# A seventh place for split weight factors, in the mixers' tile of values, and one hidden tile of FFN1's first half more by Strassen's scheme

## The chip, the cores and the metric

The kernel runs on one core of one Trainium2 chip, in one launch. The metric is the device time of an execution in microseconds. The kernel before takes 1800.26 us (median of 3 runs, 1800.17 to 1800.42).

## The reference

One step of a hybrid decoder layer: a SwiGLU FFN taken half, a mixer (a gated linear recurrence beside sliding-window attention), and a second such FFN. All is fp32. The model is 1024 wide, the FFN's hidden layer 2816; 1024 prompt tokens and 32 sample tokens are worked on.

```python
def swiglu_ffn(x, w_gate, w_up, w_down):
    return (jax.nn.silu(x @ w_gate) * (x @ w_up)) @ w_down
...
    x = x + 0.5 * swiglu_ffn(rms_norm(x, ffn1[0]), ffn1[1], ffn1[2], ffn1[3])
    y, h_last, new_conv, new_k, new_v = token_mixer(rms_norm(x, mix[0]), pos, h0, conv_buf,
                                                    k_cache, v_cache, win, mix[1:])
    x = x + y
    x = x + 0.5 * swiglu_ffn(rms_norm(x, ffn2[0]), ffn2[1], ffn2[2], ffn2[3])
```

The change touches only how the two FFNs' products are made.

## The kernel before

**Precision.** Each fp32 value is kept as a high part rounded to the matmul's type and a low part, the rest. A product then is three matmuls: high by high, high by low, low by high. Weights are split on the core: ACT copies the loaded weights into a high part, DVE subtracts it from them for the low part.

**Stages.** Tokens go in two halves, one of them 544 wide (512 and the 32 sample tokens), the other 512. The order of work on PE is: FFN1's first half (544), FFN1's second half together with the first mixer, FFN2's first half with the second mixer, FFN2's second half (544). An FFN half walks over 22 hidden tiles of 128 (f = 0 to 21): gate and up products of a tile, the evacuation to `h` = silu(gate) x up, its split; after f = 3, 6, 10, 14, 18 and at the end come the down products of a group of hidden tiles (a down block).

**Plain and Strassen.** A plain tile (`gu`) has two units of weights (gate, up), each 128 x 1024, loaded by SP as 512 KB (`raw<-w`), split by L460 (ACT) and L462 (DVE). In the 544-wide halves its matmuls go over two halves of 272 columns (L502, L503): 96 for a tile. A tile by Strassen's scheme in Winograd's form (`gu7`) takes both units at once: four loads of 256 KB (`fa<-w`, L396), four sums on DVE (L414), seven factors 128 x 512, and seven products of 12 matmuls (L936): 84 for a tile. The products come in the order P1, P5, P6, P3, P7, P2, P4. P1, P2 and P4 take loaded quarters of the weights, the other four take sums. Their inputs are four quarters of x and four sums of them, T1 to T4, made once (`factors_of`, subtractions L697, splits L676 on ACT and L678 on DVE). T4 of FFN1's first half is split only when PE has done the last plain tile: it lies over what these read. `ev7` (L883 to L892) and `copy_of` (L869) evacuate the products. FFN1's first half has `FIRST7` plain tiles and goes on by `gu7`; FFN2's second half has three plain tiles, then `gu7`, and its down blocks go by the same scheme from the second on (`down7`, L1079: 84 matmuls for two units, two pairs of units, so 168 for a block).

**The places for split factors.** `whi_t` and `wlo_t` hold six places of 512 columns, managed by `wslots`. A plain unit takes an aligned pair of them, a factor of a product a single one. `split_pair` fills a single place: the high part by ACT (L429), the low one by DVE (L437); only in FFN2's second half, where the first half has stored the low parts of the same weights to `wl` in HBM, those of P1, P2 and P4 come back by a load that POOL issues (L433, 256 KB, 87 in all). The place is free again when PE has read it for the last matmul of its product.

**Which place is taken.** `Banks._pick` decides:

```python
        if n == 2:
            c = [(max(f[i].t, f[i + 1].t), i) for i in range(0, self.n, 2) if i in f and i + 1 in f]
        else:
            c = [(i ^ 1 in f, t.t, i) for i, t in f.items()]
        return min(c) if c else None
```

For a single place the first thing compared is whether the place's partner (its number with the last bit turned) is free too; a place whose partner is in use comes first. Only then the time at which it comes free, then its number.

**What sets the order.** `Sched` runs generators that yield requests for an engine (`Req`: engine, estimated duration, what it depends on), always the one that can start first by its own estimates, and so fixes each engine's order of instructions when the kernel is built. A load from `wl` is put down there as 1.0 us on POOL and 3.5 us more to landing. On the chip the order stands and semaphores do the rest: the refill of a place waits for PE's last reader of its old contents, PE waits for the refill.

**The mixers' tile of values.** `vt` (128 x 5 x 4 x 64) holds the attention's values. It is written first at L1512 and L1519, in the mixers, and read last at L1615. In FFN1's first half and in FFN2's second half it lies unused.

Of the kernel before, what the change touches and what calls it, by code (L numbers as in the profile page):

```python
# [74 lines left out]
WARM = 10  # L75
ORDER = ((0, 1, 2, 3), (0, 1, 2, 3, "s"))
MODES = (None, "tanh", "tanh")
FIRST7 = 7
MAINCAP = 6
DBIAS = 0.8  # L80

# [142 lines left out]
def layer(ctx: ExitStack, tc, t):  # L224
# [8 lines left out]
    NBIG, NPF, NH, NRM, NRAW, NW, NMX, NLW = 26, 4, 5, 6, 2, 3, 4, 1  # L233
# [5 lines left out]
    whi_t = const.tile([128, 2 * NW, 512], F32R, name="whi")  # L239
    wlo_t = const.tile([128, 2 * NW, 512], F32R, name="wlo")  # L240
# [3 lines left out]
    vt = const.tile([128, 5, 4, 64], F32R, name="vt")  # L244
# [34 lines left out]
    raws, wslots, mxp, lws = Pool(range(NRAW)), Banks(2 * NW), Pool(range(NMX)), Pool(range(NLW))  # L279
# [128 lines left out]
    def sums(n):  # L408
# [3 lines left out]
        for i, (o, x, y, op) in enumerate(((a, u1, u2, OP.add), (b, a, g1, OP.subtract), (c, g2, b, OP.subtract), (u1, g1, u1, OP.subtract))):  # L412
            tk = yield Req("D", 0.6, tok["raw", n, 0])
            V.tensor_tensor(o, x, y, op)  # L414
            done(("sum", n, i), tk)

    def split_pair(n):

        yield Req("A", 0.0, tok["raw", n, 0])
        (g1, g2, u1, u2), (s1, s2, s3) = raw_of[n], sum_of[n]  # L420
        st, pool, names = pairs[n]
        src = {"P1": (g1, None), "P5": (s1, 0), "P6": (s2, 1), "P3": (s3, 2), "P7": (u1, 3), "P2": (g2, None), "P4": (u2, None)}
        wplace[n], left = {}, []
        for name in names:
            r, dep = src[name]
            tk = yield Req("A", 0.55, tok["raw", n, 0] if dep is None else tok["sum", n, dep], wslots.soon(), when=wslots.has())
            w = wplace[n][name] = wslots.get()
            hi, lo = whi_t[:, w], wlo_t[:, w]
            S.activation(hi, F(r, 0), AF.Copy)  # L429
            at = LO[name] if st == 3 else None  # L430
            if at:
                tkl = yield Req("G", 1.0, tok["wl", order[n + at[0]]], lat=3.5)
                G.dma_start(lo, t["wl"][order[n + at[0]] - U_FFN2, :, at[1]])  # L433
                tk = Tok(max(tk.t, tkl.t))
            else:
                tk = yield Req("D", 0.6, tk)
                V.tensor_tensor(lo, F(r, 0), f32(hi), OP.subtract)  # L437
            done(("w", n, name), tk)
            left.append(r)
            if tok["sum", n, 3].t is not None and tok["w", n, "P7"].t is not None:  # L440
                pool.put(tk, *left)
                left = []
# [335 lines left out]
    def ffn(st, g, st2, u0, mode, rslot=None, plain=NF, d7=False):  # L778
# [3 lines left out]
        w = wide(st, g)  # L782
# [114 lines left out]
        def gu7(f):  # L897

            while hs.n() < 1:
                yield Req("P", 0.0, when=hs.has())  # L900
            H[f] = hs.get()[0]
            n = unit()
            unit()
            yield Req("P", 0.0, pff.soon(2), when=pff.has(2))
            a = pff.get()[0]
            if kept(f):
                yield Req("P", 0.0, big.soon(), when=big.has())
            c = (big if kept(f) else pff).get()[0]
            bs = []
            z0, z1 = slice(0, CB), slice(CB, 2 * CB)  # L910

            plan7 = (("P1", 0, "x1a", "", ("m1", F(a, w)[:, z0])), ("P5", 1, "T1", "", ("m5", F(c, w)[:, z1])), ("P6", 0, "T2", "m1", ("mV", F(a, w)[:, z1])),
                     ("P3", 1, "x2b", "m5", None), ("P7", 0, "T3", "mV", ("mW", F(c, w)[:, z0])), ("P2", 2, "x2a", "", None), ("P4", 0, "T4", "mW", None))
            for i, (name, b, x, after, then) in enumerate(plan7):
                xs = [fx(st, x, k) for k in range(4)]
                deps = [tok["w", n, name]] + [d for _, _, d in xs]
                dur = 12 * (CB / 2400 + 0.0125)
                if after:
                    tk = yield Req("P", dur, *deps, tok[after, f])
                elif b == 0:  # L920
                    tk = yield Req("P", dur, *deps, banks.soon(), when=lambda: banks.has()() and main_out[0] < 8)
                    bs.append(banks.get())
                    main_out[0] += 1
                elif b == 1:
                    tk = yield Req("P", dur, *deps, banks.soon(2), when=lambda: banks.has(2)() and main_out[0] < 7)
                    bs += [banks.get(2)]
                    bs.insert(1, bs[1] + 1)
                    main_out[0] += 2
                else:
                    tk = yield Req("P", dur, *deps)  # L930
                wp = wplace[n][name]
                for k, (h, l, _) in enumerate(xs):
                    o = k * 128
                    wh, wl = whi_t[:, wp, o:o + 128], wlo_t[:, wp, o:o + 128]
                    for j, (u, v) in enumerate(((wh, h), (wh, l), (wl, h))):
                        PE.matmul(ps[:, bs[b], :CB], u, v, start=not after and k == j == 0, stop=k == 3 and j == 2, skip_group_check=bool(after))  # L936
                wslots.put(tk, wp)
                done((name, f), tk)
                if then:
                    sc.spawn(copy_of(bs[b], then[1], tk, then[0], f), 0)  # L940
                if i == 5:
                    sc.spawn(ev7(f, bs, a, c), 0)
            if f == NF - 1:
                xfree(st2, g)
                if st == 1 and not g:
                    xfree(1, 1)
# [98 lines left out]
        def down7(gi, i):  # L1045

            grp = GROUPS[gi]
            n = unit()
            unit()
            z0, z1 = slice(0, CB), slice(CB, 2 * CB)  # L1050
            dn, bs = [None] * 2, [[None] * 3 for _ in range(2)]
            spec = {"P1": (0, "x1a", "", "m1"), "P5": (1, "T1", "", "m5"), "P6": (0, "T2", "m1", "mV"), "P3": (1, "x2b", "m5", None),
                    "P7": (0, "T3", "mV", "mW"), "P2": (2, "x2a", "", None), "P4": (0, "T4", "mW", None)}
            for name in pairs[n][2]:
                b, x, after, then = spec[name]
                xs = [hx(grp, x, k) for k in range(2)]
                for j in range(2):
                    key = (gi, i, j)
                    deps = [tok["w", n, name]] + [d for _, _, d in xs]
                    dur = 6 * (CB / 2400 + 0.0125)  # L1060
                    if after:
                        tk = yield Req("P", dur, *deps, tok[after, key])
                    elif b == 0:
                        tk = yield Req("P", dur, *deps, banks.soon(), when=lambda: banks.has()() and main_out[0] < 8)
                        bs[j][0] = banks.get()
                        main_out[0] += 1
                    elif b == 1:
                        tk = yield Req("P", dur, *deps, banks.soon(2), when=lambda: banks.has(2)() and main_out[0] < 7)
                        bs[j][2] = banks.get(2)
                        bs[j][1] = bs[j][2] + 1  # L1070
                        main_out[0] += 2
                    else:
                        tk = yield Req("P", dur, *deps)
                    wp = wplace[n][name]
                    for k, (h, l, _) in enumerate(xs):
                        o = j * 256 + k * 128
                        wh, wl = whi_t[:, wp, o:o + 128], wlo_t[:, wp, o:o + 128]
                        for q, (u, v) in enumerate(((wh, h), (wh, l), (wl, h))):
                            PE.matmul(ps[:, bs[j][b], :CB], u, v, start=not after and k == q == 0, stop=k == 1 and q == 2, skip_group_check=bool(after))  # L1079
                    done((name, key), tk)  # L1080
                    if then:
                        to = {"m1": (0, z0), "mV": (0, z1), "mW": (1, z0), "m5": (2, z0)}[then]
                        sc.spawn(copy_of7(bs[j][b], dn, j, to, tk, then, key), 0)
                    if name == "P5":
                        sc.spawn(evd7(gi, 2 * i + j, bs[j], dn, key), 1)
                wslots.put(tk, wp)
            if i == 1:
                for f in grp:
                    hs.put(tk, H.pop(f))
# [812 lines left out]
    rslot = big.get()[0]  # L1902
    plan = ffn(1, 0, 2, 0, "late", rslot, plain=FIRST7) + merge(ffn(1, 1, 2, 0, MODES[1]), mixer(0))
    plan += merge(ffn(3, 0, 4, U_FFN2, MODES[2]), mixer(1))
# [13 lines left out]
    def free_rslot():  # L1918
        yield Req("D", 0.0, tok["s", 1, 0, FIRST7 - 1], *(tok["y", k] for k in range(4)))
        big.put(tok["s", 1, 0, FIRST7 - 1], rslot)  # L1920

# [177 lines left out]
```

## Time and profile before

| | |
|---|---|
| runs, median (3) | 1800.26 us |
| profiled execution, its own time | 1800.32 us |
| its span | 1798.3 us |
| PE busy | 1786.3 us, 11106 matmuls |
| DVE, ACT busy | 1298.0 us, 984.9 us |
| POOL's loads from `wl` | 87, 256 KB, median 3.7 us to landing |

The span goes from the first to the last instruction of the profiled execution; 2.0 us lie around it. A row of the groups names line, engine, operation, output and inputs, count, then busy time, mean ns of one, the idle time ahead and what ended most of it. In a timeline a row is the start, the length, the engine and line, and in brackets the idle time before it with what ended it. PE is the engine that is busy throughout; what another engine does costs time where PE waits for it.

### The profile page before, as it was taken

The numbers are of one execution on the slowest core, as the hardware profiler recorded it, in microseconds if no ns is written. First come the engines' busy times: TensorE is split into PE (matmuls) and PEld (weight loads), VectorE is DVE, ScalarE is ACT, GpSimd is POOL, SyncE is SP. The second block draws the span as 40 slices with busy tenths as digits, with TensorE's granted clock in tenths as the row PEclk, the third lists the DMA queues.
The fourth block names the chain that finished last, engine by engine and source line by source line (L and its number), as shares of the span: only waits on it lengthen the run. The fifth ranks groups of instructions, "written<-read, shape, count | busy, mean of one in ns | idle before, by whom it ended". The sixth has DMA issues, their size and how long they took to land.

```text
span 1798.3 us, 28694 instructions
## 1 busy us (share of the span) xinstructions
PE 1786.3 (99%) x11106; PEld 1627.8 (91%) x11106; DVE 1298.0 (72%) x2218; ACT 984.9 (55%) x1685; POOL 61.7 (3%) x134
## 2 busy tenths in 40 slices
PE   9999999999999999999999999999999999999998
PEld 9999999998888888888889898888889899999998
DVE  7877777787765687746567666875664768888887
ACT  6435445454765577423457447674542445666665
POOL 0000000010000000000000000000000001111110
PEclk9999999999999999999999999999999999999999
DMA  4232343335233322423343455444553644556563
GB/s 158 97 112 94 102 139 125 99 106 164 89 104 95 104 79 71 141 96 98 100 161 118 142 152 154 124 135 152 169 180 102 192 153 137 179 168 180 174 178 121
DMA packets 94968, 235.75 MB, mean 131 GB/s; under 512 B 11232, under 2 KB 13792, under 8 KB 94816
## 3 DMA queue, kind: packets, MB, share of 16 engines
q1 hardware_dynamic: 82160, 211.01, 36.6%
q0 software_dynamic: 12528, 22.81, 4.6%
q8 instruction: 87, 1.43, 0.3%
q14 instruction: 49, 0.40, 0.1%
q10 hardware_dynamic: 144, 0.10, 0.0%
HBM read 199.48 MB, written 32.71 MB: 129 GB/s over the span
## 4 chain that ended last, share of the span: by engine, by line
PE 97%; DVE 1%; issue 1%; DMA 0%; ACT 0%; SPq 0%; DVEq 0%; POOLq 0%
PE ps L936 20%; PE ps L492 16%; PE ps L493 15%; PE ps L494 15%; PE ps L503 11%; PE ps L502 11%; PE ps L1079 5%; PE ps L1598 1%; PE ps L1333 0%; PE ps L1560 0%; PE ps L1616 0%; PE ps L1561 0%; PE ps L1617 0%; PE ps L1449 0%; PE ps L349 0%
## 5 line engine op out<-in xcount | busy, mean ns | idle before, releaser
L460 ACT ACTIVATE whi<-raw 128x1024 fp32r<-128x1024 f32 (+1 forms) x224 | 232.0, 1036 | 316.6 <-PE ps L493 131.1
L492 PE MATMUL ps<-xh,whi 128*128 128x512 f32 x880 | 345.1, 392 | 0.0
L493 PE MATMUL ps<-xl,whi 128*128 128x512 f32 x880 | 343.1, 390 | 0.6 <-DVE xl L648 0.6
L494 PE MATMUL ps<-xh,wlo 128*128 128x512 f32 x880 | 342.9, 390 | 0.0
L462 DVE TENSOR_TENSOR wlo<-raw,whi 128x1024 fp32r<-128x1024 f32 (+1 forms) x224 | 267.4, 1194 | 80.5 <-ACT whi L460 79.4
L936 PE MATMUL ps<-xh,wlo 128*128 128x272 f32 x832 | 240.6, 289 | 0.0
L936 PE MATMUL ps<-xl,whi 128*128 128x272 f32 x832 | 239.8, 288 | 0.0
L936 PE MATMUL ps<-xh,whi 128*128 128x272 f32 x832 | 239.7, 288 | 0.0
L429 ACT ACTIVATE whi<-fa 128x512 fp32r<-128x512 f32 x308 | 189.3, 626 | 76.3 <-PE ps L503 38.5
L494 PEld LDWEIGHTS ps<-xh,wlo 128*128 128x128 f32 x880 | 165.2, 188 | 34.9
L493 PEld LDWEIGHTS ps<-xl,whi 128*128 128x128 f32 x880 | 165.3, 188 | 34.3 <-DVE xl L648 1.7
L492 PEld LDWEIGHTS ps<-xh,whi 128*128 128x128 f32 x880 | 165.2, 188 | 33.0
L437 DVE TENSOR_TENSOR wlo<-fa,whi 128x512 fp32r<-128x512 f32 x221 | 149.3, 686 | 42.1 <-ACT whi L429 41.8
L835 DVE SCALAR_TENSOR_TENSOR fa<-ps,fa 128x512 f32<-128x512 f32 (+1 forms) x152 | 106.0, 701 | 70.6 <-PE ps L494 47.4
L936 PEld LDWEIGHTS ps<-xh,whi 128*128 128x128 f32 x832 | 156.7, 188 | 0.0
L936 PEld LDWEIGHTS ps<-xl,whi 128*128 128x128 f32 x832 | 156.5, 188 | 0.0
L936 PEld LDWEIGHTS ps<-xh,wlo 128*128 128x128 f32 x832 | 156.5, 188 | 0.0
L492 PE MATMUL ps<-ha,whi 128*128 128x512 f32 x352 | 138.2, 393 | 0.7 <-ACT whi L460 0.4
L493 PE MATMUL ps<-ha,whi 128*128 128x512 f32 x352 | 137.3, 390 | 0.3 <-DVE ha L1108 0.3
L494 PE MATMUL ps<-ha,wlo 128*128 128x512 f32 x352 | 137.2, 390 | 0.0
L414 DVE TENSOR_TENSOR fa<-fa 128x512 f32<-128x512 f32 x176 | 117.7, 685 | 6.0 <-DMA fa<-w 5.1
L869 ACT ACTIVATE fa<-ps 128x272 f32<-128x272 f32 x136 | 54.1, 398 | 97.2 <-PE ps L936 95.9
(302 smaller groups left out, 3771.0 us busy)
## 6 DMA issues: line engine op xcount, KB each, us to landing
raw<-w SPq DMA_DIRECT2D x216, 512.0 KB, 3.4
fa<-w SPq DMA_DIRECT2D x180, 256.0 KB, 3.9
wlo<-wl POOLq DMA_DIRECT2D x87, 256.0 KB, 3.7
wl<-wlo SPq DMA_DIRECT2D x29, 512.0 KB, 5.0
wl<-wlo SPq DMA_DIRECT2D x29, 256.0 KB, 4.2
fa<-x SPq DMA_DIRECT2D x16, 256.0 KB, 2.7
fa<-x SPq DMA_DIRECT2D x8, 272.0 KB, 4.4
xs<-fa SPq DMA_DIRECT2D x8, 272.0 KB, 4.4
```

What stands on the lines that cost most here:

```text
L414: V.tensor_tensor(o, x, y, op)
L429: S.activation(hi, F(r, 0), AF.Copy)
L437: V.tensor_tensor(lo, F(r, 0), f32(hi), OP.subtract)
L460: S.activation(hi, raw, AF.Copy)
L462: V.tensor_tensor(lo, raw, f32(hi), OP.subtract)
L492: PE.matmul(p, wh, ah, start=first, stop=False)
L493: PE.matmul(p, wh, al, start=False, stop=False)
L494: PE.matmul(p, wl, ah, start=False, stop=last)
L502: PE.matmul(ps[:, b, :CB], w, a[:, c0], start=s, stop=e)
L503: PE.matmul(ps[:, b + 1, :CB], w, a[:, c1], start=s, stop=e)
L835: V.scalar_tensor_tensor(x, P_(b, w), fac, x, op0=OP.mult, op1=OP.add)
L936: PE.matmul(ps[:, bs[b], :CB], u, v, start=not after and k == j == 0, stop=k == 3 and j == 2, skip_group_check=bool(after))
```

## The change

```diff
-FIRST7 = 7
+FIRST7 = 6
...
+    wslots.free[2 * NW] = Tok(0.0)
+
+    def w_at(w):
+        if w < 2 * NW:
+            return whi_t[:, w], wlo_t[:, w]
+        y = vt.rearrange("p a b c -> p (a b c)")
+        return y[:, :512], y[:, 512:1024]
...
             w = wplace[n][name] = wslots.get()
-            hi, lo = whi_t[:, w], wlo_t[:, w]
+            hi, lo = w_at(w)
             S.activation(hi, F(r, 0), AF.Copy)
...
-                    wh, wl = whi_t[:, wp, o:o + 128], wlo_t[:, wp, o:o + 128]
+                    wh, wl = (y[:, o:o + 128] for y in w_at(wp))
...
-                        wh, wl = whi_t[:, wp, o:o + 128], wlo_t[:, wp, o:o + 128]
+                        wh, wl = (y[:, o:o + 128] for y in w_at(wp))
```

A seventh place, number 6, lies in `vt`: high parts in its first 512 columns, low parts in the next 512. It can be taken as a single place by a factor of a product in `gu7` (the first pair of changed lines in the loops) and in `down7` (the second), so in FFN1's first half and in FFN2's second. Pairs are sought among the first six alone. Place 6 would have number 7 as its partner, which doesn't exist. Hidden tile f = 6 of FFN1's first half goes from plain to Strassen's scheme. PE's order is otherwise the same by line; the lines behind L416 move down by nine (L429 becomes L438, L437 L446, L433 L442, L936 L945, L1079 L1088).

The orders of ACT and DVE move. The first place is in FFN2's second half, at the end of the third down block and the start of the tile behind it, on ACT. `raw<-ps` are copies of the down block's products, `fa<-ps` those of the tile's (`copy_of`), `whi<-fa` and `vt<-fa` the high parts of factors. Before:

```order
L429 ACTIVATE whi<-fa 128x512 x2
L1000 ACTIVATE raw<-ps 128x272 x2
L429 ACTIVATE whi<-fa 128x512 x2
L869 ACTIVATE fa<-ps 128x272
L429 ACTIVATE whi<-fa 128x512
L869 ACTIVATE fa<-ps 128x272
L429 ACTIVATE whi<-fa 128x512
L869 ACTIVATE fa<-ps 128x272
L429 ACTIVATE whi<-fa 128x512 x5
```

After:

```order
L438 ACTIVATE whi<-fa 128x512
L438 ACTIVATE vt<-fa 128x512
L1009 ACTIVATE raw<-ps 128x272 x2
L438 ACTIVATE whi<-fa 128x512 x2
L438 ACTIVATE vt<-fa 128x512
L878 ACTIVATE fa<-ps 128x272 x3
L438 ACTIVATE vt<-fa 128x512
L438 ACTIVATE whi<-fa 128x512 x4
L438 ACTIVATE vt<-fa 128x512
```

The vt place is filled again and again in this stretch, once with only three copies of products between two fills, and the splits that stood between the tile's copies now stand behind them.

The second place is DVE in FFN1's first half, where f = 6 begins: `fa<-ps,fa` at L825 (L834 after) is the end of the evacuation of f = 5, L678 (L687) the low parts of T factors (`xl<-fa,xh` T4's), L414 the sums of a tile's weights, L1221 and on the mixers' constants. Before:

```order
L802 TENSOR_TENSOR fa<-fa 128x544
L678 TENSOR_TENSOR xl_67<-fa,xh_65 128x272
L678 TENSOR_TENSOR kb<-fa,kb 128x272
L678 TENSOR_TENSOR rm<-fa,rm 128x272
L697 TENSOR_TENSOR fa<-fa 128x272
L1221 TENSOR_SCALAR mxt<-mxt 128x4
L1222 TENSOR_SCALAR mxt<-mxt 128x4
L1223 RECIPROCAL mxt<-mxt 128x4
L1224 TENSOR_TENSOR mxt<-mxt 128x4
L1227 TENSOR_TENSOR mxt<-mxt 128x4 x3
L825 TENSOR_TENSOR fa<-ps,fa 128x544
```

After:

```order
L811 TENSOR_TENSOR fa<-fa 128x544
L687 TENSOR_TENSOR rm<-fa,rm 128x272
L706 TENSOR_TENSOR fa<-fa 128x272
L414 TENSOR_TENSOR fa<-fa 128x512 x3
L834 TENSOR_TENSOR fa<-ps,fa 128x544
L446 TENSOR_TENSOR wlo<-fa,whi 128x512
L687 TENSOR_TENSOR xl_66<-fa,xh_64 128x272 x2
L1117 TENSOR_TENSOR ha<-fa,ha 128x544
L687 TENSOR_TENSOR xl_66<-fa,xh_64 128x272
L446 TENSOR_TENSOR vt<-fa,vt 128x512
L687 TENSOR_TENSOR xl_66<-fa,xh_64 128x272
```

Sums of f = 6's weights stand where the constants stood, and the low parts of its factors and T4's follow behind the evacuation of f = 5; the constants come later.

## The prediction

> **What bounds the kernel now.** I read the page first, then PE's waits, the chain in order of time, the windows, and the landing times of the `wl` loads. The page says that TensorE is the bound:
>
> ```profile
> span 1798.3 us, 28694 instructions
> PE 1786.3 (99%) x11106; PEld 1627.8 (91%) x11106; DVE 1298.0 (72%) x2218; ACT 984.9 (55%) x1685; POOL 61.7 (3%) x134
> PE 97%; DVE 1%; issue 1%; DMA 0%; ACT 0%; SPq 0%; DVEq 0%; POOLq 0%
> ```
>
> PE works in 1786.3 of 1798.3 us and makes 97% of the chain. So a change is worth what it does to PE: matmuls fewer or more, and waits fewer or more. The waits of PE (line, what was waited for, total, times, longest) are very few:
>
> ```profile
> PE ps L1079 <- DMA wlo<-wl: 1.9, 1, 1.9
> PE ps L1189 <- DVE rm L1187: 1.7, 1, 1.7
> PE ps L502 <- DVE fa L835: 0.8, 1, 0.8
> ```
>
> The longest is a wait for a low half that POOL loads from `wl`, once, at the end of FFN2's second half. Everything else arrives in time, and the six places for split factors are what gives it that time: a place is refilled while PE reads from the others. The change touches just that.
>
> **Price of one matmul.** In the chain in order of time two unbroken stretches of FFN2's second half give it, 336 products of the gate and up tiles (L936) and 168 of a down block (L1079):
>
> ```profile
> 1526.46 21.18 PE ps L1079 x168
> 1547.64 42.23 PE ps L936 x336
> ```
>
> 42.23/336 = 0.1257 us, 21.18/168 = 0.1261 us; I use the first.
>
> **Part 1, FIRST7 7 to 6.** Hidden tile f=6 of FFN1's first half has 96 plain matmuls of 272 columns and gets 84. That is 12 x 0.1257 = 1.5 us off PE, which is on the path: **-1.5 us**. ACT and DVE get seven splits, four sums and the evacuation of `ev7` for two wide splits. That costs nothing if they hide beside PE. The narrowest place is there, since T4, f=6's sums and its splits now come in f=6's own stretch. DVE is loaded here:
>
> ```profile
> 50.00:100.00 50.00, 49.15 (x392) 48.97 (x391) 45.17 (x105) 20.72 (x39) 0.00 (x0) 1.00 0.27 88
> 90.93 0.43 DVE L678 TENSOR_TENSOR rm<-fa,rm 128x272 fp32r<-128x272 f32 x1
> 93.34 0.72 DVE L825 TENSOR_TENSOR fa<-ps,fa 128x544 f32<-128x544 f32 x1 [0.22 <-PE ps L503]
> 105.37 0.72 DVE L825 TENSOR_TENSOR fa<-ps,fa 128x544 f32<-128x544 f32 x1 [3.24 <-PE ps L503]
> 109.03 1.49 DVE L678 TENSOR_TENSOR xl<-fa,xh 128x272 fp32r<-128x272 f32 x4
> L437 DVE TENSOR_TENSOR wlo<-fa,whi 128x512 fp32r<-128x512 f32 x221 | 149.3, 686 | 42.1 <-ACT whi L429 41.8
> L414 DVE TENSOR_TENSOR fa<-fa 128x512 f32<-128x512 f32 x176 | 117.7, 685 | 6.0 <-DMA fa<-w 5.1
> ```
>
> (The first row is a window: its length, then busy time and count of PE, PEld, DVE, ACT and POOL.) DVE is busy 45.17 of 50 us. PE ends f=5 at about 93.2, where the first L825 starts; the next comes 12.03 us later, after f=6. The factors before T4 are done by 91.4 (first row of L678). P4, the product that needs T4, would be PE's seventh, 72 matmuls or 9.1 us after 93.2, at 102.3. Four T4 splits (1.49), three or four sums and seven lows (0.69 each) are some 9 us of DVE work, of which a part stands ahead of 93.2 in the new order. Walking the new DVE order with these durations I get each low 1 to 2 us ahead of its product. I take 0, and +3 us as the other end, DVE's idle 3.24 us being the cover used up.
>
> **Part 2, the seventh place: what it does in FFN2's second half.** `_pick` takes for a single a place whose partner isn't free, before it looks at the time. Place 6 has no partner, so it is always taken first when free; of the pairs, broken ones come before whole ones. Through the end of each down block, where no more than three places are asked for, the new order fills only three in turn (the vt place and two others), while two pairs stand idle. I read from the two built orders the place of every split and of its readers on PE. Before, a refill has 62 matmuls (7.8 us) from the last read of the old contents to the first read of the new low half, 36 at the least, and 14 only at the very tail. After, at the ends of the four down blocks (after f=6, 10, 14, 18; in before's time near 1545, 1608, 1672 and 1736 us) three loads in succession (P2, P4 and the next product's P1) have 26, as have one P2 and one P4 in tiles behind the first and fourth block, and P2 and P4 at the tail: 26 x 0.1257 = 3.27 us.
>
> What such a refill takes shows at the one place where the lead is short already:
>
> ```profile
> 1786.10 0.41 PE L1079 MATMUL ps<-rm,whi 128*128 128x272 f32 x2
> 1787.61 0.41 PE L1079 MATMUL ps<-ha,whi 128*128 128x272 f32 x2
> 1789.88 0.39 PE L1079 MATMUL ps<-ha,wlo 128*128 128x272 f32 x1 [1.86 <-DMA wlo<-wl]
> 1790.36 0.28 PE L1079 MATMUL ps<-ha,wlo 128*128 128x272 f32 x1
> 1786.67 0.54 POOL L433 DMA_DIRECT2D wlo<-wl  x1 [13.17 <-PE ps L1079]
> 1786.67 3.16 DMA wlo<-wl
> ```
>
> The last reader starts at 1786.10, POOL issues at 1786.67 (0.57 later), the load takes X = 3.16, PE starts 0.04 after its landing. Unhindered, PE would have read at 1787.61 + 2 x 0.1257 = 1787.86, 14 matmuls after 1786.10; it starts 2.02 late. So a refill by POOL costs PE W = 0.61 + X - lead: with 26 matmuls W = X - 2.66, with 62 never anything.
>
> X by the landing times of L433, for all 87, in 100 us of the stretch, and in three windows of three loads each (min/median/max), and the issues of one such three:
>
> ```profile
> DMA to landing us min/median/max: 2.7/3.7/7.0
> DMA to landing us min/median/max: 2.8/4.0/5.3
> DMA to landing us min/median/max: 3.0/4.1/4.7
> DMA to landing us min/median/max: 3.7/4.6/5.4
> DMA to landing us min/median/max: 3.1/3.4/3.7
> ```
>
> ```profile
> 1558.66 0.53 POOL L433 DMA_DIRECT2D wlo<-wl  x1 [7.00 <-PE ps L936]
> 1560.16 0.53 POOL L433 DMA_DIRECT2D wlo<-wl  x1 [0.98 <-DVE wlo L437]
> 1561.67 0.53 POOL L433 DMA_DIRECT2D wlo<-wl  x1 [0.98 <-PE ps L936]
> ```
>
> (The first is the whole run, then 1500 to 1600, 1537 to 1541, 1622 to 1626, 1695 to 1700.) Of the three loads of a group the slowest decides: the three are issued 1.5 us apart, one a product, and a wait at the first moves the second and third reads as well. In the 18 windows of three that I asked for the slowest takes 3.7 to 5.4 (the last two rows are the ends) and 4.7 on average. W = 4.7 - 2.7 = 2.0, four times: **+8.0 us**. The two lone ones go by the median: 3.7 - 2.66 = 1.04 each, **+2.1**. At the tail the lead grows from 14 to 26 and the old wait of 2.02 becomes 3.16 - 2.66 = 0.5: **-1.5**.
>
> By the Trainium skill (DMA: Bandwidth & Descriptors, Anatomy of one DMA, SWDGE path) a load issued by GpSimd takes 2.0 us plus its bytes over 436 GB/s, an estimate of 2.6 us for 256 KB; by it W is 0 at every group and the sum below is some 10 us less. The rows disagree: 2.7 is the least of 87 loads and the median is 3.7.
>
> **Lows that DVE makes.** P5, P6, P3 and P7 are refilled through ACT and DVE instead:
>
> ```profile
> 1783.16 0.63 ACT L429 ACTIVATE whi<-fa 128x512 fp32r<-128x512 f32 x1
> 1783.83 0.69 DVE L437 TENSOR_TENSOR wlo<-fa,whi 128x512 fp32r<-128x512 f32 x1 [0.36 <-ACT whi L429]
> 131.18 0.40 ACT L869 ACTIVATE fa<-ps 128x272 f32<-128x272 f32 x1 [1.13 <-PE ps L936]
> 131.47 0.62 ACT L429 ACTIVATE whi<-fa 128x512 fp32r<-128x512 f32 x1
> ```
>
> From ACT's start to the end of the low half is 1.36 us; within 3.27 that leaves 1.6 for a queue, so nothing. One exception: in the tile behind the third down block (near 1679) P3 takes the vt place that P6, the product right ahead of it, has just read. Its high split stands behind P6's copy (L869): 0.29 + 0.67 + 0.69, less 0.25 for the two matmuls that need only the high half, is about 1.4, with the start of the chain 1.6: **+1.6 us**. Bounds: 1.3 (the bare chain) to 2.5 (one more DVE instruction ahead).
>
> **Sum.** -1.5 + 8.0 + 2.1 - 1.5 + 1.6 = **+8.7 us**. The profiled execution took 1800.32 (2.0 around the span of 1798.3), the median of the runs is 1800.26: so **1809.0 us**. A measurement of this kernel can tell about 0.2%, 3.6 us, from no change: 1796.7 to 1803.9.
>
> Ends: with every X at the median of 3.7 the groups cost 4 x 1.04 and the sum is 4.2 + 2.1 + 1.6 - 3.0 = +4.9 (1805.2); with 5.4 at every group, 4 x 2.74, it is +11.7 (1812); with 2.8 everywhere, 4 x 0.14 + 2 x 0.14 + 1.6 - 1.5 - 1.9 = -1.0 (1799.3).
>
> **Rivals.**
>
> *A, not slower: the loads land within the lead.* The places are fewer in use, but a load of 2.8 us would still make 26 matmuls, and then only the matmuls saved and P3's wait remain: -1.0, 1799.3 us. For it: the one load at the tail took 3.16, when traffic is light, and the least is 2.7. The Trainium skill's estimate of 2.6 us, above, would give this case. Against it: the groups lie in the busiest stretch,
>
> ```profile
> 1500.00:1700.00 200.00, 200.00 (x1592) 199.99 (x1592) 174.71 (x315) 131.58 (x270) 30.16 (x57) 1.00 0.58 174
> 1786.10:1793.00 6.90, 5.03 (x38) 4.55 (x36) 2.82 (x6) 1.95 (x4) 1.07 (x2) 1.00 0.36 116
> ```
>
> where DMA engines are busy 0.58 against 0.36 at the tail, and move 174 GB/s against 116. It decides where the slowest of three stays under about 3.2. 12%.
>
> *B, f=6's factors come late.* PE then waits in FFN1's first half too, up to 3 us: 1812. For it: DVE's 90% in that window; against: the 1 to 2 us ahead. 12%.
>
> *C, the clock falls after the waits.* After 1.86 us of wait one matmul takes 0.39 and the next are at 0.28 or 0.29 again, and the granted clock in that window is 1.00. The Trainium skill (TensorE: Matmul & The Clock Gate, Part 1) has the clock halved after an idle window of about 3.4 us; no wait of before is so long, so none here shows it. Were 14 matmuls behind each of six waits at twice 0.1257, that would be 6 x 1.8 = 10.6 more, 1820. My waits are 2 us: 3%.
>
> *D, faster.* Only if the groups don't wait, P3's wait doesn't come either and the tail's wait goes: -1.5 - 2.0 = -3.5, at the very edge, 1796.8. 3%.
>
> The forecast has the remaining 70%. Range 1800.0 to 1813.5: its lower end leaves out D and most of A, its upper end takes in 5.4 at every group and half of B. Chances: faster 0.03; same 0.12; slower 0.85, from the forecast, B and C.
>
> **What would show it.** Right: among PE's waits L1088 (the down blocks) and L945 (the tiles) on `wlo` or `vt` loads, some six to nine times, 8 to 11 us in all, in groups 63 us apart; PE's matmuls 12 fewer; a tail wait of about 0.5; no wait near 93 to 105 us; L945 once for vt's low by DVE near 1685. Wrong: PE's waits as short as before with a span near 1797 (A or D); waits on `fx` tiles or lows of DVE in the first 110 us (B); matmul durations of 0.4 and more behind the waits (C).

## The result and the profile after

The changed kernel takes 1820.22 us (median of 4 runs, 1816.44 to 1822.35); the kernel before takes 1800.34 (4 runs, 1800.17 to 1800.69). The ratio is 1.0107, with a 95% interval of 1.0095 to 1.0119: slower by 19.9 us. The forecast was 1809.0 with a range up to 1813.5, so the direction was right and the size less than half of what came. The runs of the changed kernel also scatter over 5.9 us, some ten times as much as those of before.

The profiled execution took 1820.77 us. The head of its page, then the share of its chain by engine:

```profile
span 1819.0 us, 28666 instructions
PE 1792.8 (99%) x11094; PEld 1631.1 (90%) x11094; DVE 1301.9 (72%) x2228; ACT 980.7 (54%) x1690; POOL 61.7 (3%) x134
...
PE 93%; DVE 2%; issue 2%; DMA 2%; ACT 0%; POOL 0%; SPq 0%; DVEq 0%; POOLq 0%; ACTq 0%
```

PE has twelve matmuls less to do (x11106 became x11094) and yet is busy for 6.5 us more. That points to matmuls that ran slower, though a wait too lengthens the matmul behind it (0.39 us where the next takes 0.28, in the rows of the tail in the prediction). The waits of PE after:

```profile
PE ps L1088 <- DMA wlo<-wl: 5.9, 5, 2.4
PE ps L945 <- DMA vt<-wl: 3.6, 2, 3.0
PE ps L1088 <- DMA vt<-wl: 3.4, 2, 2.0
PE ps L1198 <- DVE rm L1196: 1.7, 1, 1.7
PE ps L945 <- ACT vt L438: 1.0, 1, 1.0
PE ps L511 <- DVE fa L844: 0.8, 1, 0.8
PE ps L945 <- DMA wlo<-wl: 0.6, 1, 0.6
```

Ten waits for loads from `wl`, 13.5 us in all, where there was one of 1.9. Where they lie is read from the chain in order of time, at the start of FFN2's second half and at those of its down blocks. After:

```profile
1470.48 10.57 PE ps L945 x84
...
1524.80 13.65 PE ps L1088 x108
...
1594.33 4.54 PE ps L1088 x37
...
1660.43 13.65 PE ps L1088 x108
...
1728.55 13.64 PE ps L1088 x108
...
1790.73 2.28 PE ps L1088 x18
```

The same places before (the second of them, 1526.46, stands in the prediction):

```profile
1472.14 10.57 PE ps L936 x84
...
1589.87 21.17 PE ps L1079 x168
...
1653.26 21.19 PE ps L1079 x168
...
1716.68 21.17 PE ps L1079 x168
...
1769.54 9.96 PE ps L1079 x78
```

The differences of the starts are -1.66, -1.66, +4.46, +7.17, +11.87 and +21.19 us, and the span ends +20.7. Up to FFN2's second half the change has won 1.7 us. Each down block with the tiles behind it then loses 6.1, 2.7, 4.7 and 9.3 us, and the tail wins 0.5. These rows put all of the loss in one stage.

### The profile page after: what moved, and what is told of

Its sections match the earlier page's. It is cut to its first block, busy times and chain, and to the rows that moved or that the text cites. A ratio compares the mean times of both kernels' runs of the same rounds, so it can differ in the third digit from the quotient of the medians.

```text
span 1819.0 us, 28666 instructions
## 1 busy us (share of the span) xinstructions
PE 1792.8 (99%) x11094; PEld 1631.1 (90%) x11094; DVE 1301.9 (72%) x2228; ACT 980.7 (54%) x1690; POOL 61.7 (3%) x134
## 4 chain that ended last, share of the span: by engine, by line
PE 93%; DVE 2%; issue 2%; DMA 2%; ACT 0%; POOL 0%; SPq 0%; DVEq 0%; POOLq 0%; ACTq 0%
PE ps L945 19%; PE ps L501 15%; PE ps L502 15%; PE ps L503 15%; PE ps L512 11%; PE ps L511 10%; PE ps L1088 3%; DMA vt<-wl 1%; DMA wlo<-wl 1%; PE ps L1607 1%; PE ps L1342 0%; PE ps L1569 0%; PE ps L1625 0%; PE ps L1570 0%; PE ps L1626 0%
## 5 line engine op out<-in xcount | busy, mean ns | idle before, releaser
L945 PE MATMUL ps<-xh,wlo 128*128 128x272 f32 x716 | 208.1, 291 | 0.6 <-DMA wlo<-wl 0.6
L945 PE MATMUL ps<-xh,whi 128*128 128x272 f32 x716 | 207.4, 290 | 0.0
L945 PE MATMUL ps<-xl,whi 128*128 128x272 f32 x716 | 207.3, 290 | 0.0
L503 PEld LDWEIGHTS ps<-xh,wlo 128*128 128x128 f32 x880 | 165.2, 188 | 34.9
L502 PEld LDWEIGHTS ps<-xl,whi 128*128 128x128 f32 x880 | 165.3, 188 | 34.3 <-DVE xl L657 1.7
L501 PEld LDWEIGHTS ps<-xh,whi 128*128 128x128 f32 x880 | 165.2, 188 | 32.9
L438 ACT ACTIVATE whi<-fa 128x512 fp32r<-128x512 f32 x249 | 151.6, 625 | 45.1 <-PE ps L512 23.8
L446 DVE TENSOR_TENSOR wlo<-fa,whi 128x512 fp32r<-128x512 f32 x183 | 123.3, 687 | 37.3 <-ACT whi L438 36.9
L945 PEld LDWEIGHTS ps<-xh,wlo 128*128 128x128 f32 x716 | 135.6, 189 | 1.0 <-DMA wlo<-wl 1.0
L945 PEld LDWEIGHTS ps<-xh,whi 128*128 128x128 f32 x716 | 136.1, 190 | 0.1
L945 PEld LDWEIGHTS ps<-xl,whi 128*128 128x128 f32 x716 | 135.9, 190 | 0.0
L414 DVE TENSOR_TENSOR fa<-fa 128x512 f32<-128x512 f32 x180 | 120.4, 686 | 8.4 <-DMA fa<-w 7.0
```

The source lines that it names most:

```text
L501: PE.matmul(p, wh, ah, start=first, stop=False)
L502: PE.matmul(p, wh, al, start=False, stop=False)
L503: PE.matmul(p, wl, ah, start=False, stop=last)
```

## The experiments

Times of before are 1800.11, 1800.54 and 1800.32 us in the three sets of runs.

### Which half of the change

`e1_ffn1_only` withdraws place 6 when FFN2's second half begins, `e2_ffn2_only` hands it out only there and leaves `FIRST7` at 7:

```diff
         st, pool, names = pairs[n]
+        if st == 3:
+            wslots.free.pop(2 * NW, None)
```

> The seventh place is withdrawn before FFN2's second half; FFN1's first half keeps it, with f=6 by Strassen's scheme. Theory (the loss is made in FFN2's second half, by refills whose lead fell from 62 to 26 matmuls): the waits on wl loads go but for the old one at the tail, and what stays is part 1, 12 matmuls less: 1800.3 - 1.6 = 1798.7 us. Rival (FFN1's late factors, or the new orders of ACT and DVE in the mixers, make the loss): 1815 us or more.

> The reverse: FIRST7 stays 7, and the seventh place is handed out only from FFN2's second half on. Theory: all of the loss, and without the 1.6 us of part 1: 1820.2 + 1.6 = 1821.8 us (1817 to 1825, as its executions scatter), with waits at the ends of the same four down blocks. Rival: about 1800.3 us.

Measured: e1 1798.59 us (ratio 0.9992, 0.9983 to 1.0001), e2 1817.74 us (1.0096, 1.0081 to 1.0112). e1's first row of waits is that of before again:

```profile
PE ps L1090 <- DMA wlo<-wl: 1.9, 1, 1.9
```

In e2 PE waits for loads eleven times, 12.0 us in all. So the loss is made in FFN2's second half and by the seventh place. e1 stands 1.5 us under its before, the price of twelve matmuls, though a difference of that size isn't proven by its interval. e2 stays 4 us under its forecast of 1821.8, within the range that was given.

### The place, or the rule that picks it

`e4_time_first` keeps both parts of the change and mends the pick. `Banks` also hands out the eight PSUM banks (`banks`), so this edit changes how those are picked as well:

```diff
-            c = [(i ^ 1 in f, t.t, i) for i, t in f.items()]
+            c = [(t.t, i) for i, t in f.items()]
```

> The change as it is, seventh place in both stages, but _pick takes the single place that comes free first, without looking at its partner. In the built order no refill by POOL then has a lead under 40 matmuls, at the tail neither. Theory (which place is taken makes the loss, not that it lies in vt): no waits on wl loads, the tail's old wait of 2.0 us gone as well: 1800.3 - 1.6 - 2.0 = 1796.7 us. Rival (a place in vt is dear in itself, by its refills or its reads): vt is used more often here, so 1815 us or more.

Measured: 1795.79 us, ratio 0.9976 (0.9967 to 0.9984). All of PE's waits over 0.3 us:

```profile
PE ps L1198 <- DVE rm L1196: 1.7, 1, 1.7
PE ps L511 <- DVE fa L844: 0.8, 1, 0.8
PE ps L502 <- DVE xl L657: 0.6, 2, 0.4
```

No wait for `wl` is left, neither at the blocks nor at the tail, with vt in fuller use than in the change. So a place in vt costs nothing that shows in PE's waits. This is faster than both kernels. The start of FFN2's second half lies at 1468.72 us here, 1.8 earlier than in the changed kernel, and the span is 25.2 us shorter. So some 23 us are won in that stage, where the waits for loads are gone; the 1.8 lie in the stages before it, whose orders the edit changes too, and single executions differ there by about 1 us (e4 and e13, the same kernel).

`e3_last_choice` ranks place 6 between: as if its partner were always free. It leaves the PSUM banks alone, since none of them has the number `self.n`.

```diff
-            c = [(i ^ 1 in f, t.t, i) for i, t in f.items()]
+            c = [(i ^ 1 in f or i == self.n, t.t, i) for i, t in f.items()]
```

> The change with another rank for place 6: it counts as a place whose partner is free, so that broken pairs still come first, then the earliest of the rest. In the built order P2 and P4 at the ends of the second, third and fourth down block have a lead of 26 matmuls, the P1 behind them 38, the first block, the tiles behind the blocks and the tail none under 38. Theory: three waits of 5.3 - 2.66 = 2.6 us, the clock lowered behind one or two of them at 1.5 us each, part 1 and the tail's wait gone: 1800.1 + 7.9 + 2.2 - 1.6 - 2.0 = 1806.6 us (1803 to 1810). Rival (any use of place 6 costs, or only place 6's refills): under 1798, or 1815 and more.

Measured: 1808.15 us, ratio 1.0040 (1.0025 to 1.0055), with 7.4 us of waits:

```profile
PE ps L1088 <- DMA wlo<-wl: 7.4, 5, 2.1
```

Between the two, as the leads are: fewer short leads, fewer waits. The loss follows the refills with 26 matmuls of lead, not the seventh place as such.

### Is it the landing of the load

`e5_pool_sub` leaves the short leads and takes the load out: POOL subtracts instead.

```diff
-                G.dma_start(lo, t["wl"][order[n + at[0]] - U_FFN2, :, at[1]])
+                G.tensor_tensor(lo, F(r, 0), f32(hi), OP.subtract)
```

> The change with its short leads of 26 matmuls (3.27 us), but where POOL loads a low part from wl, it subtracts on chip instead (weights less their high part, 128x512). Theory (lead less landing time makes the wait): the refill takes ACT's 0.65 us and POOL's subtraction in place of 0.6 + 5.3 us; if POOL takes under 2 us for it the groups don't wait: 1800.3 - 1.6 + 1.6 (P3's wait stays) - 1.9 = 1798.4 us, up to 1803 if POOL is slower or gets in DVE's way. Rival (the wait is for the place, or PE's clock falls for another reason, whatever fills it): 1815 us or more.

Measured: 1834.92 us, ratio 1.0194 (1.0181 to 1.0208). That lies where the rival put it, but not for the rival's reason; the theory had POOL in DVE's way, and priced it far too low. The waits for loads are gone, but others came:

```profile
PE ps L945 <- ACT fa L878: 9.7, 11, 2.5
PE ps L945 <- DVE fa L1024: 3.8, 2, 1.9
...
PE ps L945 <- POOL wlo L442: 0.3, 1, 0.3
```

POOL's subtractions (shortest, median, longest in ns), one sum of weights on DVE, and the load of DVE over 200 us of this stage (length, then busy time and count of PE, PEld, DVE, ACT, POOL), tell why:

```profile
L442 POOL TENSOR_TENSOR wlo<-fa,whi x66: 1282/1494/2377, 1475.0 to 1821.8; 128x512 fp32r<-128x512 f32 x66
```

```profile
L414 DVE TENSOR_TENSOR fa<-fa 128x512 f32<-128x512 f32 x63 | 59.9, 973 | 0.3
```

```profile
1500.00:1700.00 200.00, 185.15 (x1410) 180.97 (x1410) 192.69 (x279) 111.65 (x236) 73.46 (x49) 0.98 0.27 87
```

The same sum takes 973 ns on average beside POOL's work where it took 685 before, and DVE is busy 192.7 of 200 us, where it had been 174.7 (PE: 185.2). DVE became the busiest engine of this stage. PE's only direct wait for a POOL refill is 0.3 us, so a refill that is short enough does fit the lead; but the time of this kernel says nothing of the theory, since the experiment moved the bound. What ties the waits to the landings is the trace of the changed kernel itself: at each of its ten waits for loads PE goes on 0.04 us after the load has landed (the first long one lands at 1541.86 + 5.20 = 1547.06, and PE goes on at 1547.10).

### Does the clock fall after a wait

Three stretches of this stage in the changed kernel's profile have matmuls 0.23 us apart instead of 0.126. Windows of some 3.4 us over the wait and behind it, in pairs, for the waits that end at 1547, 1617, 1767 and 1751 (the column behind POOL's is the granted clock):

```profile
1544.57:1547.99 3.42, 1.40 (x12) 1.18 (x11) 1.08 (x3) 0.63 (x1) 0.00 (x0) 1.00 0.58 175
1547.99:1551.40 3.41, 3.41 (x18) 3.41 (x17) 3.31 (x7) 1.15 (x2) 0.00 (x0) 0.51 0.00 0
1612.83:1616.25 3.42, 1.66 (x12) 1.44 (x12) 1.90 (x3) 1.76 (x4) 1.58 (x3) 1.00 0.79 225
1616.25:1619.66 3.41, 2.93 (x23) 2.93 (x24) 1.81 (x4) 0.00 (x0) 0.53 (x1) 1.00 0.55 176
1763.00:1766.55 3.55, 0.66 (x6) 0.45 (x4) 2.12 (x4) 1.03 (x2) 0.53 (x1) 1.00 1.04 276
1766.55:1769.97 3.42, 3.33 (x15) 3.33 (x16) 0.66 (x2) 0.63 (x1) 0.00 (x0) 0.50 0.62 202
1749.40:1752.80 3.40, 1.49 (x12) 1.49 (x12) 0.51 (x2) 0.00 (x0) 0.00 (x0) 1.00 0.62 180
1752.80:1756.30 3.50, 3.50 (x18) 3.50 (x17) 2.85 (x5) 1.48 (x3) 0.00 (x0) 0.51 0.03 5
```

The granted clock is halved behind three of the four, for about 3.4 us each. `e8_gaps` tests that on the kernel before with waits made on purpose:

```diff
+            if name == "P4" and n in gaps:
+                yield Req("A", 0.0, tok["copied", 3, "mW", gaps[n]])
...
             S.activation(hi, F(r, 0), AF.Copy)
+            if name == "P4" and n in gaps:
+                for _ in range((2, 3, 4, 5, 6)[gaps[n] % 5]):
+                    tk = yield Req("A", 0.55)
+                    S.activation(hi, f32(hi), AF.Copy)
```

> The kernel before, in which P4 of each of the 19 tiles of FFN2's second half that go by Strassen's scheme waits on purpose: its high half is made only after the copy of P7's product, and copied onto itself two to six more times (the value stays). PE then waits between about 0.8 and 3.5 us at P4, in turn, some 41 us in all, and now and then for a load. If PE's clock falls only after 3.4 us of idle time, at most the longest of these waits are followed by matmuls 0.23 us apart: about 1800 + 41 + 4 = 1845 us. If a wait of about 2 us suffices when it fills over half of one of the clock gate's free-running windows, waits under 1.8 us are never followed by slow matmuls, those of 2 to 3 us in about half of the cases, and each time the slow stretch ends at the same phase of a period of 3.4 us: 8 to 12 times 1.5 us, about 1855 us.

In this kernel some evacuations of products come ahead of work whose results they take, so part of FFN2's output is worked out from other numbers; the matmuls and their sizes are those of before. Measured: 1898.55 us (1896.86 to 1900.24). The time is 43 us over the higher forecast, in the main because the waits came out longer than planned (up to 4.5 us, 66 us in all); what counts is each wait and what stands behind it. Two waits of 2.1 us, each with a window of some 3.4 us behind it:

```profile
1539.06:1541.15 2.09, 0.00 (x0) 0.00 (x1) 1.99 (x5) 1.96 (x5) 0.53 (x1) 1.00 0.52 176
1542.40:1545.80 3.40, 3.40 (x17) 3.40 (x16) 2.21 (x5) 1.03 (x2) 0.00 (x0) 0.51 0.28 80
1660.35:1662.45 2.10, 0.00 (x2) 0.00 (x1) 1.99 (x5) 1.97 (x5) 0.53 (x1) 1.00 0.52 162
1662.45:1665.90 3.45, 3.45 (x27) 3.45 (x28) 3.42 (x8) 2.16 (x5) 0.53 (x1) 1.00 0.50 167
```

Waits of the same length: one is followed by 17 matmuls in 3.4 us at clock 0.51, the other by 27 at 1.00. Over all 33 waits of this stage that are over 0.3 us: none of the 16 up to 1.2 us is followed by slow matmuls, five of the nine from 2.0 to 2.8 us are, and all eight from 3.2 to 4.5 us. The slow stretches end at 1487.72, 1545.80, 1678.89, 1794.90 and so on. From 1545.80 to 1678.89 are 39 periods of 3.413 us, to 1794.90 are 73: all 13 ends lie within 0.3 us of one phase of that period. Laid into this grid, each wait falls on one side: where the idle part inside one period is 2.04 us or more, the clock falls (13 times); where it is 1.86 us or less, it doesn't (20 times). The ends fix the grid to some 0.2 us only, so the limit is about 2 us. In the profile of the changed kernel the limit lies at the same place, between 1.8 and 2.0 us, with two waits too near to it to tell.

The Trainium skill (TensorE: Matmul & The Clock Gate, Part 1) has a free-running window of 3413 ns, which these ends bear out, and lets the clock fall after one idle window; here a window some 55 to 60% idle was enough.

### What else the places are worth

`e12` and `e10` (run again as `e14`) are the kernel before, six places, with the time-first rule and `FIRST7` at 7 and at 6; `e13` is e4 again; `e9` is e4 with `FIRST7 = 5`.

> The kernel before with FIRST7 = 6 and the time-first rule of _pick, without the seventh place and vt. No refill by POOL has a lead under 40 matmuls, at the tail neither. Theory (the rule decides, the seventh place gives nothing beyond it): as e4, 1795.8 us within 1. Rival (the seventh place is what gives f=6's factors and the tail their time): 1798 us or more, with PE waits near 93 to 105 us or at the tail.

> The kernel before with the time-first rule alone: six places, FIRST7 = 7, vt untouched. Theory: only the tail's wait of 2.0 us goes, about 1798.2 us where the kernel before takes 1800.2. If the rule gains elsewhere too (e4 was 0.7 us under its forecast), 1797.5 us or less. Rival (without the seventh place or without f=6 by Strassen's scheme the rule does nothing): 1800 us.

> e4 once more (seven places, time-first rule, FIRST7 = 6), beside the next one on the same chip: 1795.8 us.

> e10 once more (six places, time-first rule, FIRST7 = 6). If the seventh place is worth nothing once the rule is mended, within 0.5 us of the run beside it; if it is worth something, 1 us or more above it.

> Seven places, time-first rule, and FIRST7 = 5: one more hidden tile by Strassen's scheme. Theory: another 12 x 0.1257 = 1.5 us less than e4: 1794.3 us, if the factors of x are there when PE comes to f=5, 12 us earlier. Rival (DVE can't make the factors by then, rival B of the prediction): PE waits near 81 us and the time is 1796 us or more.

| kernel | places, FIRST7 | us | ratio, 95% interval |
|---|---|---|---|
| e12 | 6, 7 | 1797.12 | 0.9981 (0.9973 to 0.9990) |
| e10 | 6, 6 | 1796.13 | 0.9975 (0.9966 to 0.9984) |
| e14 | 6, 6 | 1796.49 | 0.9978 (0.9970 to 0.9987) |
| e13 | 7, 6 | 1795.90 | 0.9974 (0.9963 to 0.9984) |
| e9 | 7, 5 | 1801.27 | 1.0003 (0.9994 to 1.0012) |

The rule alone gives 3.2 us of the 4.4, more than the tail's 2.0. FFN2's second half starts earlier in e12's profiled execution than before (1472.14):

```profile
1469.13 10.57 PE ps L936 x84
```

By the starts in this execution, which is 1.1 us faster than e12's median, 3.0 us are won ahead of the stage that the argument was about, some 2.2 at its tail, and 1.0 is lost at its down blocks. The edit changes the pick of the places and that of the PSUM banks; which of the two wins the 3.0, less what the execution gives by chance, was not tried.

f=6 by Strassen's scheme gives 0.6 us more (e14), and the seventh place another 0.6 (e13), which can't be told from nothing. One tile further, the gain is gone: e9 waits at f=5 and its neighbours (71 to 104 us), where DVE is late. The two largest rows:

```profile
PE ps L945 <- DVE vt L446: 2.0, 1, 2.0
PE ps L945 <- DVE xl L687: 2.0, 2, 1.3
```

## Why the prediction was right in direction and wrong in size

Two steps of the prediction failed. Its term X, the time from issue to landing, was too small: the waits for loads ahead of the tail cost 15.2 us where the sum had 8.0 + 2.1. And it put the clock at nothing, on the ground that waits of 2 us are too short for it to fall: it fell three times, for 4.5 us.

**Part 1 held.** Forecast -1.5 us and no wait for f=6's factors; the starts of FFN2's second half differ by -1.66, and among the waits there is none in FFN1's first half that before hadn't. Rival B was false for f=6 and true one tile earlier (e9).

**The place and the mechanism held.** The waits lie at the four down blocks, the two tiles and P3 that the orders had named. e1 and e2 show that the loss is made by the seventh place in FFN2's second half, e3 and e4 that it goes with the rule that picks it. P3 behind P6 cost 1.3 us of waits by two rows, 1.85 us from start to start, against +1.6:

```profile
1690.04 0.39 PE L945 MATMUL ps<-xh,vt 128*128 128x272 f32 x1 [1.00 <-ACT vt L438]
...
1690.87 0.52 PE L945 MATMUL ps<-xh,vt 128*128 128x272 f32 x2 [0.32 <-DVE vt L446]
```

**The term X was too small.** The prediction took 4.7 for a group, the mean of the slowest of three loads, and the median of 3.7 for the lone ones. The landings in the chain after, for the P4 loads of the first three groups and the lone P4 behind the fourth:

```profile
1541.86 5.20 DMA vt<-wl
...
1611.38 5.31 DMA wlo<-wl
...
1677.49 5.35 DMA vt<-wl
...
1760.81 5.79 DMA vt<-wl
```

The P4 load of the fourth group, issued at 1745.60, took 5.67. W = X - 2.66 itself held: from start to start PE lost 2.4, 2.6, 2.6 and 2.9 us at the four groups (the small wait at P2 and the long one at P4 together), where the formula gives 2.5, 2.7, 2.7 and 3.0, and 3.1 at the lone P4, where it gives 3.1. So the law was right, and its X was taken from loads that the change then made later: in the kernel before, the same four P4 loads took 4.7, 3.5, 3.8 and 4.7 us.

A third lone refill, P4's behind the first block, was not on the prediction's list. Its load stood behind P2's on POOL:

```profile
1555.08 0.53 POOL L442 DMA_DIRECT2D vt<-wl  x1 [11.19 <-DVE wlo L446]
1555.66 1.14 POOL L442 DMA_DIRECT2D wlo<-wl  x2
```

The P4 load is the first of the second row. It starts right behind its neighbour with no wait of its own, since POOL issued its loads in the built order and the neighbour's place, read by P6 just before, had come free only then. The prediction had counted the leads from the place alone. This load took 5.19 us, and PE waited for it too.

From start to start the groups cost 10.4 us (8.0 forecast) and the loads behind the first and fourth block 4.8 (2.1 forecast): 15.2 us, 5.1 more. Why the loads land later than before is not shown. While the four groups' P4 loads were under way, the DMA engines were busy 0.85 to 0.98 and moved 246 to 278 GB/s; over the same four loads before it was 0.80 to 0.84 and 224 to 237. So crowding is likely, but leaving out other loads was not tried.

**Rival C came true in its mechanism and had been given 3%.** It had 1.8 us for each fall of the clock, "after an idle window of about 3.4 us", and was kept out of the sum since "My waits are 2 us". That condition was wrong: waits of 2.0, 2.4 and 3.0 us lowered the clock, one of 2.2 didn't. In 3.4 us 27 matmuls fit, at half the clock 15; the 12 lost are 1.5 us, three times 4.5 us. That C's total of 1820 lies so near the measured 1820.2 is luck: it counted six falls, there were three, and longer waits made up the rest.

The clock also fits the scatter, though this was not tested: in e8 it hung on a wait's place in the period whether a wait of 2 us lowered the clock. The four runs have mean clocks of 0.997, 0.998, 0.995 and 0.997 at 1820.8, 1816.4, 1822.4 and 1819.7 us: the lowest clock with the longest time, the highest with the shortest. By estimate a fall takes half of 3.41 us, 0.001, off the mean clock, so the two ends differ by about three falls, 4.5 of the 5.9 us.

**The tail** saved 0.5 and not 1.5: the wait for `wl` fell from 1.86 to 0.2 us, but a split of h on DVE took 0.37 and other small ones followed. That is 1.0 us of the error.

**The sum.** The span grew by 20.7 us (1819.0 less 1798.3), against +8.7. Of the 12.0 us between, 5.1 are longer waits, 4.5 the clock, 1.0 the tail and 0.2 P3; part 1 gave back 0.2. The remaining 1.4 is about what starting again after a wait costs: where the clock didn't fall, the first matmul takes 0.23 us to the next one instead of 0.126, and that came eleven times.

## What to carry to other kernels

A buffer added to a pool helps only as far as the rule that hands it out lets it: look in the built order for how long each refill has between the last reader and the next, and count the queue that issues it, not the buffer alone. A place that is always preferred shortens the rotation to the preferred ones. Price a wait on TensorE with the clock it may cost: one of 2 us can cost 3.5.

## What the runs showed of the hardware

- The clock was halved for about one period of 3.41 us behind a period in which PE idled for about 2 us or more (13 waits, 2.04 and up), and not where it idled less (20 waits, up to 1.86; all in e8). A wait of 2.1 us fell on either side by its phase alone.
- POOL's subtraction of 128x512 beside DVE's work took 1.28 to 2.38 us, and DVE's sums of that size went from 685 to 973 ns (e5).
- Loads of 256 KB from `wl` landed later in the changed kernel, median 4.4 us where it was 3.7 before, with the same bytes to move:

```profile
DMA to landing us min/median/max: 2.8/4.4/6.7
```
